# A feed-forward split in two parts by tokens: 384 tokens with plain products, 768 with Strassen's seven half-size products in the up projection

## The chip, the core and the metric

The kernel runs on one core of one Trainium2 chip, as one launch. The metric is the device time of that launch in microseconds, the median of three runs. The core's engines work in parallel, each through its own list of instructions in order: TensorE (PE, matrix products into PSUM), VectorE (DVE), ScalarE (ACT), GpSimd (POOL), and SyncE (SP), which issues the DMA transfers here.

## The reference, cut to what matters

One step of a hybrid backbone layer on 1024 latent tokens and 128 prompt tokens: a mixer (a bidirectional mLSTM branch beside a grouped-query attention branch), then a feed-forward of width 4096 on a model width of 1024. All is float32. The change is in the feed-forward, the second half of the layer:

```python
    x = layer_norm(ALPHA * x + g1 * mix, ln1_g, ln1_b)
    h = x * (1 + sc2) + sh2
    ff = jnp.square(jax.nn.relu(h @ w_up)) @ w_down
    x = layer_norm(ALPHA * x + g2 * ff, ln2_g, ln2_b)
```

`w_up` is 1024 x 4096 and `w_down` 4096 x 1024; `sh2`, `sc2` and `g2` come from a conditioning vector, one set for the latent tokens and one for the prompt.

## The kernel before, in words

The 1152 tokens are 9 tiles of 128 (eight latent, the last one the prompt), gathered in three groups of 384 for products that have tokens as columns. The program has four stages: input projection and mLSTM, attention, branch and output projections with the first layer norm, feed-forward.

Every float32 product is made of three: `split` (L69 to L71) copies an operand to a rounded high part on ScalarE (L70) and takes the difference as a low part on VectorE (L71); `mm3` (L73 to L78) multiplies high by high (L76), high by low (L77, L78). A weight goes through `wslot`: a load of 512 KB into one of the two `raw` buffers of the pool `rp`, then a split into one of four pairs of slots `wh`, `wl` of the pool `wp`. The next load into a `raw` buffer waits until both halves of the split, or whatever else reads it, are done.

The feed-forward runs over 16 blocks of 256 hidden columns. `up(fb)` (L1111) loads and splits 1024 x 256 of w_up (`w_pair`, two slots), and for each of three token groups and two halves of 128 hidden columns makes one PSUM tile u by 24 matmuls of 384 columns: 144 in a block. ScalarE takes relu out of PSUM (L1122), VectorE squares it (L1123), and a split gives the tiles ah and al. `down(fbs, parts, last)` (L1130) loads and splits 256 rows of w_down, and for each of 9 token tiles and two halves of the model width makes a tile d by 6 matmuls of 512 columns, 108 in a block, which VectorE adds to acc in SBUF (L1143; in the first block a copy, L1141). PSUM has three buffers for u and three for d. The loop is up(fb + 1), then down(fb), so that the vector work on one block's activations lies beside the next block's products.

The modulated, transposed activations h2T (high and low, one pair of tiles th, tl for each group of 384) stay in SBUF throughout. In the last block `residual` (L1158) turns acc into ALPHA * x1 + g2 * acc, with x1 loaded back from DRAM, one buffer of 512 KB. The last down takes blocks 14 and 15 together, 12 matmuls a tile; it scales by g2 (L1146), adds (L1147), takes statistics (L1148) and, one token tile behind, finishes the layer norm (`finish`, L1170: ScalarE L1179, VectorE L1180, GpSimd L1181, store).

The order of instructions on each engine is settled when the kernel is built, by a scheduler that goes by the program's dependencies, the pools' buffers and its own estimates of durations. So an operation may stand far from the place at which the program's text has it.

Of the kernel before, what the change touches and what calls it, by code (L numbers as in the profile page):

```python
# [12 lines left out]
ALU = mybir.AluOpType  # L13
# [21 lines left out]
def hybrid_step_kernel(  # L35
# [15 lines left out]
    def pool(stack, name, bufs=1, **kw):  # L51
        return stack.enter_context(tc.tile_pool(name=name, bufs=bufs, reuse_waits="tile", **kw))
# [10 lines left out]
    def load(out, in_):  # L63
        nc.sync.dma_start(out=out, in_=in_)
# [32 lines left out]
    def kview(w):  # L97
        return w.rearrange("(k p) n -> p k n", p=128)
# [860 lines left out]
    st3r = ctx.enter_context(ExitStack())  # L959
    st3 = ctx.enter_context(ExitStack())  # L960
    ps3t = pool(st3r, "ps3t", 2, space=PSUM, side="right")
# [95 lines left out]
        nc.gpsimd.tensor_tensor(out=y, in0=y, in1=gain, op=ALU.mult)  # L1057
# [18 lines left out]
    h2T = []  # L1076
    for s in range(NT):
        if s in (0, NS):
# [16 lines left out]
        x1s.append(xt)  # L1095
        if s:
            modulate2(s - 1)
    st3.close()

# [1 line left out]
    st4 = ctx.enter_context(ExitStack())  # L1101
    ps4 = pool(st4, "ps4", 3, space=PSUM)
    fp = pool(st4, "fp", 1)

    def ft(shape, tag, bufs=1, ty=F32):
        return fp.tile(list(shape), ty, tag=tag, bufs=bufs, name=tag)

    NFB = DFF // 256
    wdv = kview(w_down)

    def up(fb, mid=None, each=None):  # L1111
        w = w_pair(w_up, 256 * fb)
        ah = ft([128, 2, 1152], "ah", 2, F32R)
        al = ft([128, 2, 1152], "al", 2, F32R)
        for b in range(NTB):
            for m in range(2):
                if (b, m) == (1, 1) and mid:
                    mid()
                g = ps4.tile([128, 512], F32, tag="u", name="u4")
                mm3(g[:, 0:TB], [(w[m][k], (h2T[b][0][:, k, :], h2T[b][1][:, k, :])) for k in range(KT)])  # L1120
                r = ft([128, 512], "r", 2)[:, 0:TB]
                nc.scalar.activation(out=r, in_=g[:, 0:TB], func=AF.Relu)  # L1122
                nc.vector.tensor_tensor(out=r, in0=r, in1=r, op=ALU.mult)  # L1123
                sl = slice(b * TB, b * TB + TB)
                split(ah[:, m, sl], al[:, m, sl], r)
                if each:
                    each()
        return ah, al

    def down(fbs, parts, last):  # L1130
        ws = [(a, m, wslot([(0, wdv[:, 2 * fb + m:2 * fb + m + 1, :])], 1024)) for fb, a in zip(fbs, parts) for m in range(2)]
        for s in range(NT):
            ts_ = slice(128 * s, 128 * s + 128)
            if last:
                st = ft([128, 2, 6], "bst", 2)
            for half in range(2):
                cs = slice(512 * half, 512 * half + 512)
                g = ps4.tile([128, 512], F32, tag="d", name="d4")
                mm3(g[:], [((a[0][:, m, ts_], a[1][:, m, ts_]), (w[0][:, 0, cs], w[1][:, 0, cs])) for a, m, w in ws])
                if fbs[0] == 0:  # L1140
                    nc.vector.tensor_copy(out=acc[:, s, cs], in_=g[:])  # L1141
                elif not last:
                    nc.vector.tensor_tensor(out=acc[:, s, cs], in0=acc[:, s, cs], in1=g[:], op=ALU.add)  # L1143
                else:
                    tm = ft([128, 512], "r", 2)
                    nc.vector.tensor_tensor(out=tm[:], in0=g[:], in1=g2t[0 if s < NS else 1][:, cs], op=ALU.mult)  # L1146
                    nc.vector.tensor_tensor(out=acc[:, s, cs], in0=acc[:, s, cs], in1=tm[:], op=ALU.add)  # L1147
                    nc.vector.bn_stats(out=st[:, half, :], in_=acc[:, s, cs])  # L1148
            if last:
                if s:  # L1150
                    finish(s - 1, *fin)
                fin = ln_stats(st, ft)
        if last:
            finish(NT - 1, *fin)

    g2t = []

    def residual(s):  # L1158
        if not g2t:
            for g in range(2):  # L1160
                t = ft([128, D], f"g2{g}")
                load(t[:], gmod[1, g, :].partition_broadcast(128))
                g2t.append(t)
        x1 = ft([128, D], "x1")
        load(x1[:], x1d[s][:])
        y = acc[:, s, :]
        nc.vector.tensor_tensor(out=y, in0=y, in1=g2t[0 if s < NS else 1][:], op=ALU.mult)  # L1167
        nc.vector.scalar_tensor_tensor(out=y, in0=x1[:], scalar=ALPHA, in1=y, op0=ALU.mult, op1=ALU.add)  # L1168

    def finish(s, mv, rs):  # L1170
        out = y_sample[0, 128 * s:128 * s + 128, :] if s < NS else y_prompt[0]
        nmu = ft([128, 1], "nmu", 2)
        nc.vector.tensor_scalar(nmu[:], mv[:, 0:1], -1.0, None, ALU.mult)
        n = 1 if s < NS else 2
        for i in range(n):
            w = D // n
            cs = slice(w * i, w * i + w)
            y = acc[:, s, cs]
            nc.scalar.activation(out=y, in_=y, func=AF.Identity, bias=nmu[:])  # L1179
            nc.vector.scalar_tensor_tensor(out=y, in0=y, scalar=rs[:], in1=l2g[:, cs], op0=ALU.mult, op1=ALU.mult)  # L1180
            (nc.gpsimd if s < NS else nc.vector).tensor_tensor(out=y, in0=y, in1=l2b[:, cs], op=ALU.add)  # L1181
            store(out[:, cs], y)

    a = up(0, lambda: modulate2(NS))
    st3r.close()
    st4r = ctx.enter_context(ExitStack())
    accp = pool(st4r, "accp", 1, side="right")
    acc = accp.tile([128, NT, D], F32, name="acc")
    for fb in range(NFB - 2):
        nxt = up(fb + 1)  # L1190
        down([fb], [a], False)
        a = nxt
    todo = list(range(NT))

    def some():
        for _ in range(2):
            if todo:
                residual(todo.pop(0))

    b = up(NFB - 1, None, some)  # L1200
    while todo:
        some()
    l2 = tp.tile([128, 2, D], F32, tag="t", name="l2")
    l2g, l2b = l2[:, 0, :], l2[:, 1, :]
    load(l2g, ln2_g[0].partition_broadcast(128))
    load(l2b, ln2_b[0].partition_broadcast(128))
    down([NFB - 2, NFB - 1], [a, b], True)


# [48 lines left out]
```

## Time and profile before

| what | value |
|---|---|
| runs | 2469.79, 2470.90, 2470.94 us; median 2470.9 |
| the profiled execution's span | 2469.1 us |
| busy: TensorE, VectorE, ScalarE, GpSimd | 97%, 57%, 34%, 13% |
| first matmul of an up product | at 1651.6 us |
| one feed-forward block in mid-stage | 49.51 us |
| last matmul | at 2452.0 us |
| DMA | 264.77 MB, 107 GB/s over the span |

A row of the timeline has start, duration, engine, line, operation, output and inputs, and in brackets the idle time before it with what ended it. A row of the groups has line, engine, operation, shapes and count, then busy us and mean ns of one, then idle us before them with the releasers. A row of the windows has the stretch, its length, busy us of PE, PEld, DVE, ACT and POOL, the granted TensorE clock, the DMA share and GB/s. Matmuls are pipelined, so the durations listed for them overlap; their starts tell what one costs.

### The profile page before, as it was taken

To read this page: it belongs to the slowest core of one execution; us is meant where nothing else is said; L and a number is where in the kernel's file an instruction comes from. 1 tells how busy PE (TensorE), PEld (TensorE's weight loads), DVE (VectorE), ACT (ScalarE), POOL (GpSimd) and SP (SyncE) were. 2 spreads that over 40 slices of the span, in tenths; PEclk is the share of its full clock that TensorE was granted. 3 is DMA by queue.
4 is the path that set the end of the run, shared out by engine and by line. 5 is a ranking of instruction groups with operands and counts; after the bars stand their busy time and mean duration, and the time that the engine had idled before them with its cause. 6 is when DMAs were issued, how large, how long until landed. Compare 5 with 4: busy or idle time off the path is not lost. (4 is left out here: it accounts for less than half of the span.)

```text
span 2469.1 us, 35511 instructions
## 1 busy us (share of the span) xinstructions
PE 2387.7 (97%) x13485; PEld 2163.7 (88%) x13485; DVE 1399.7 (57%) x2625; ACT 843.8 (34%) x1844; POOL 312.3 (13%) x514
## 2 busy tenths in 40 slices
PE   6999998999999899899999999999999999999997
PEld 4888887788899899889999999888999899989985
DVE  5645635645654464378787345674445444544488
ACT  3323423534433243266666333132221122212221
POOL 1001100211110010134442000230000000000004
PEclk9999999999999999999999999999999999999998
DMA  7264447445654642520001655241111111111131
GB/s 266 87 206 152 148 120 198 138 125 146 196 165 145 183 148 95 104 72 17 16 16 58 216 188 189 93 141 35 52 35 52 35 52 35 51 35 52 35 120 77
DMA packets 211162, 264.77 MB, mean 107 GB/s; under 512 B 23760, under 2 KB 157984, under 8 KB 210992
## 3 DMA queue, kind: packets, MB, share of 16 engines
q1 hardware_dynamic: 210992, 262.51, 34.7%
q8 instruction: 106, 1.74, 0.3%
q14 instruction: 64, 0.52, 0.1%
HBM read 197.23 MB, written 65.21 MB: 106 GB/s over the span
## 5 line engine op out<-in xcount | busy, mean ns | idle before, releaser
L76 PE MATMUL g<-th,wh 128*128 128x384 f32 x1088 | 373.5, 343 | 8.7 <-DVE fm L246 8.7
L78 PE MATMUL g<-th,wl 128*128 128x384 f32 x1088 | 368.3, 338 | 0.0
L77 PE MATMUL g<-tl,wh 128*128 128x384 f32 x1088 | 366.7, 337 | 0.0
L70 ACT ACTIVATE wh<-raw 128x1024 fp32r<-128x1024 f32 x148 | 154.9, 1058 | 405.8 <-PE d L78 289.4
L76 PE MATMUL u<-th,wh 128*128 128x384 f32 x768 | 256.8, 335 | 0.8 <-ACT th L70 0.8
L77 PE MATMUL u<-tl,wh 128*128 128x384 f32 x768 | 256.7, 334 | 0.6 <-DVE tl L71 0.6
L78 PE MATMUL u<-th,wl 128*128 128x384 f32 x768 | 256.7, 334 | 0.0
L76 PE MATMUL g<-wh,th 128*128 128x512 f32 x600 | 241.1, 402 | 0.0
L77 PE MATMUL g<-wl,th 128*128 128x512 f32 x600 | 236.1, 394 | 0.7 <-DVE wl L71 0.7
L78 PE MATMUL g<-wh,tl 128*128 128x512 f32 x600 | 236.5, 394 | 0.0
L1143 DVE TENSOR_TENSOR acc<-acc,d 128x512 f32<-128x512 f32 x234 | 159.4, 687 | 119.6 <-PE d L78 119.6
L77 PE MATMUL d<-wl,ah 128*128 128x512 f32 x576 | 224.6, 390 | 2.3 <-DVE wl L71 2.3
L76 PE MATMUL d<-wh,ah 128*128 128x512 f32 x576 | 224.4, 390 | 1.8 <-DVE r L1146 1.6
L78 PE MATMUL d<-wh,al 128*128 128x512 f32 x576 | 224.4, 390 | 0.0
L76 PEld LDWEIGHTS g<-th,wh 128*128 128x128 f32 x1088 | 206.3, 190 | 17.5 <-DVE fm L246 9.0
L71 DVE TENSOR_TENSOR wl<-raw,wh 128x1024 fp32r<-128x1024 f32 x148 | 180.8, 1230 | 71.2 <-ACT wh L70 70.6
L78 PEld LDWEIGHTS g<-th,wl 128*128 128x128 f32 x1088 | 206.1, 189 | 0.4 <-issue 0.4
L77 PEld LDWEIGHTS g<-tl,wh 128*128 128x128 f32 x1088 | 206.4, 190 | 0.1
L1123 DVE TENSOR_TENSOR r<-r 128x384 f32<-128x384 f32 x96 | 53.5, 558 | 166.4 <-ACT r L1122 166.3
L76 PEld LDWEIGHTS u<-th,wh 128*128 128x128 f32 x768 | 144.1, 188 | 1.7 <-ACT th L70 1.1
L77 PEld LDWEIGHTS u<-tl,wh 128*128 128x128 f32 x768 | 144.2, 188 | 1.5 <-DVE tl L71 1.0
L78 PEld LDWEIGHTS u<-th,wl 128*128 128x128 f32 x768 | 144.1, 188 | 0.0
(307 smaller groups left out, 4675.4 us busy)
## 6 DMA issues: line engine op xcount, KB each, us to landing
raw<-in_w_in_dram SPq DMA_DIRECT2D x44, 512.0 KB
kvt<-kvd SPq DMA_DIRECT2D x64, 257.0 KB
raw<-in_w_mod_dram SPq DMA_DIRECT2D x32, 512.0 KB
raw<-in_w_up_dram SPq DMA_DIRECT2D x32, 512.0 KB
raw<-in_w_down_dram SPq DMA_DIRECT2D x32, 512.0 KB
kvd<-kvs SPq DMA_DIRECT2D x36, 257.0 KB
uw<-ud SPq DMA_DIRECT2D x72, 128.0 KB
bs<-st SPq DMA_DIRECT2D x32, 258.0 KB
```

The costliest lines, as they stand in the source:

```text
L70: nc.scalar.activation(out=hi, in_=src, func=AF.Copy)
L71: nc.vector.tensor_tensor(out=lo, in0=src, in1=f(hi), op=ALU.subtract)
L76: nc.tensor.matmul(out, lhsT=ah, rhs=bh, start=start and i == 0, stop=False)
L77: nc.tensor.matmul(out, lhsT=ah, rhs=bl, start=False, stop=False)
L78: nc.tensor.matmul(out, lhsT=al, rhs=bh, start=False, stop=stop and i == n - 1)
L1123: nc.vector.tensor_tensor(out=r, in0=r, in1=r, op=ALU.mult)
L1143: nc.vector.tensor_tensor(out=acc[:, s, cs], in0=acc[:, s, cs], in1=g[:], op=ALU.add)
```

## The change

The helper lines of split become L71 to L73 and those of mm3 L78 to L80, since two constants come in above them; apart from stage 3's order of tokens, only stage 4 differs.

**Token order.** Stage 3 takes the tiles in the order 0, 1, 2, 6, 7, 8, 3, 4, 5.

**First part, tokens 0 to 2.** `up_plain` (L1194) has 48 matmuls a block, and down 36. Two up blocks precede the first down. All 16 blocks run so, the last two downs together, and the three tokens are finished then, in mid-kernel, with `residual` and `finish` as parameters of which accumulator and pool they use.

**Activation forms.** Between, `act_forms` prepares the seven activation matrices of Strassen's scheme for the other 768 tokens: a11 and a12 are the two halves in depth of the middle token group, s1 and s4 overwrite the halves of the last group, s2, s3 and a22 get tiles of their own. GpSimd adds high to low for each quarter (L1121) and subtracts (L1127), 32 operations of 128 x 384 in all, and ScalarE and VectorE split the 16 results.

**Second part, tokens 3 to 8.** All 16 blocks of w_up and w_down are loaded and split again. `up_forms` makes the seven weight forms of a block from two raw halves: GpSimd combines (L1281, four operations of 128 x 512), and each form is split into one of three rotating places of the tile uf. `up_halves` (L1330) makes seven products of 12 matmuls of 384 columns, 84 a block, in PSUM banks x, y and z; x and y have one buffer each, z is one of u's three. VectorE makes sums out of PSUM (L1339), GpSimd one (L1361), ScalarE relu and square (L1325, L1326). `down` has 72 matmuls a block, and the last of them finishes six tokens.

**Residual.** acc times g2 goes from VectorE to GpSimd (L1132), x1 is loaded in halves of 256 KB.

The core of the diff:

```diff
+NFB = 16
+SORD = (0, 1, 2, 6, 7, 8, 3, 4, 5)
...
+        for k in range(4):
+            full = []
+            for nm in ("a11", "s1", "a12", "s4"):
+                t = mk([128, TB], "v" + nm)
+                nc.gpsimd.tensor_tensor(out=t[:], in0=f(acts[nm][0][:, k, :]), in1=f(acts[nm][1][:, k, :]), op=ALU.add)
+                full.append(t)
+                yield
+            b11, b12, b21, b22 = full
+            t3 = mk([128, TB], "vs3")
+            for dst, x, y, nm in ((t3, b22, b12, "s3"), (b11, b12, b11, "s1"), (b22, b22, b11, "s2"), (b21, b21, b22, "a22")):
+                nc.gpsimd.tensor_tensor(out=dst[:], in0=x[:], in1=y[:], op=ALU.subtract)
+                split(acts[nm][0][:, k, :], acts[nm][1][:, k, :], dst[:])
+                yield
...
+    def some_forms():
+        next(forms, None)
+        next(forms, None)
+
+    T0 = (0, 1, 2)
+    for fb in range(NFB - 3):
+        down(fat, acc0, T0, [fb], [a], down_w([fb]), None, None, False)
+        a, nxt = nxt, up_plain(fb + 2, some_forms)
...
+    ORDER = ("a11", "s2", "s1", "s3", "s4", "a12", "a22")
+    BANK = "xyzyzxy"
...
+        s1 = comb(0, a21, a22, ALU.add)
+        s2 = comb(1, s1, a11, ALU.subtract)
+        yield form(a11)
+        yield form(s2)
+        yield form(s1)
+        s3 = comb(2, a11, a21, ALU.subtract)
+        yield form(s3)
+        s4 = comb(3, a12, s2, ALU.subtract)
+        yield form(s4)
+        yield form(a12)
+        yield form(a22)
...
+            for k in range(4):
+                for i, (x, y) in enumerate(((wh, bh), (wh, bl), (wl, bh))):
+                    nc.tensor.matmul(o, lhsT=x[:, k, :], rhs=y[:, k, :], start=fresh and k == 0 and i == 0,
+                                     stop=k == 3 and i == 2, skip_group_check=True)
+            if j == 0:
+                nc.scalar.activation(out=tmp("u1"), in_=o, func=AF.Copy)
+            elif j == 1:
+                tsum(tmp("u2"), u["u1"], o)
+            elif j == 2:
+                nc.scalar.activation(out=tmp("v"), in_=o, func=AF.Copy)
+            elif j == 3:
+                u3 = ft([128, TB], "r", 2)[:]
+                tsum(u3, u["u1"], o)
+                nc.gpsimd.tensor_tensor(out=u["v"], in0=u3, in1=u["v"], op=ALU.add)
+                half_out(a, 1, 1, u["v"])
...
+    for fb in range(NFB - 2):
+        nxt = up_halves(pre, aa[(fb + 1) % 2], lambda: None)
+        ws = down_w([fb])
+        pre = up_begin(fb + 2)
+        down(ft, acc, T1, [fb], [a], ws, None, None, False)
+        a = nxt
```

Three places of the order matter below. The first is VectorE at the second down product of the feed-forward; before, the add of its first group (d4_18517) stands behind the square of the last hidden half (r_18500) and two weight splits:

```order
L71 TENSOR_TENSOR al_18324<-r_18470,ah_18323 128x384
L71 TENSOR_TENSOR wl_18664<-raw_18661,wh_18663 128x1024
L71 TENSOR_TENSOR wl_18670<-raw_18667,wh_18669 128x1024
L1123 TENSOR_TENSOR r_18500<-r_18500 128x384
L1143 TENSOR_TENSOR acc_17960<-acc_17960,d4_18517 128x512
L71 TENSOR_TENSOR al_18324<-r_18500,ah_18323 128x384
```

In the changed kernel, the same place (the add of the first group of down(1) is d4_18088; va, vs are GpSimd's combined activations, tf and tl the low parts of the forms):

```order
L73 TENSOR_TENSOR tl_17342<-va11_18616,th_17341 128x384
L73 TENSOR_TENSOR al_18007<-r_18033,ah_18006 128x384
L73 TENSOR_TENSOR tfs3l_17747<-vs3_18758,tfs3h_17746 128x384
L73 TENSOR_TENSOR wl_18139<-raw_18136,wh_18138 128x1024
L73 TENSOR_TENSOR tfs2l_17745<-vs4_18652,tfs2h_17744 128x384
L73 TENSOR_TENSOR tfa22l_17749<-va12_18650,tfa22h_17748 128x384
L1203 TENSOR_TENSOR r_18067<-r_18067 128x384
L1170 TENSOR_TENSOR acc0_17930<-acc0_17930,d4_18088 128x512
L73 TENSOR_TENSOR wl_18145<-raw_18142,wh_18144 128x1024
L73 TENSOR_TENSOR al_18007<-r_18067,ah_18006 128x384
L1170 TENSOR_TENSOR acc0_17930<-acc0_17930,d4_18096 128x512
```

The splits of activation forms have moved in ahead of the square and the add. On ScalarE, at the same place of the changed kernel, the relu that feeds that square stands behind the split of the fourth s1 quarter:

```order
L72 ACTIVATE wh_18138<-raw_18136 128x1024
L72 ACTIVATE tfs2h_17744<-vs4_18652 128x384
L72 ACTIVATE tfa22h_17748<-va12_18650 128x384
L72 ACTIVATE th_17341<-va11_18905 128x384
L1202 ACTIVATE r_18067<-u4_18042 128x384
```

Ahead of it stand splits that need all but the last four of GpSimd's 32 operations. The third place is VectorE in a block of the second part, from the last activations of an up product into the adds of a down product (raw_21884 is half of a W_down block, wth the weight forms s1 and s2):

```order
L1339 TENSOR_TENSOR u1_21519<-u1_21519,psy_21524 128x384
L73 TENSOR_TENSOR uf_19924<-wth_21650,uf_19924 128x512 x2
L1170 TENSOR_TENSOR acc_20113<-acc_20113,d4_21660 128x512
L73 TENSOR_TENSOR aal_20109<-r_21629,aah_20108 128x384
L1170 TENSOR_TENSOR acc_20113<-acc_20113,d4_21668 128x512
L73 TENSOR_TENSOR wl_21887<-raw_21884,wh_21886 128x1024
L1170 TENSOR_TENSOR acc_20113<-acc_20113,d4_21676 128x512
L1170 TENSOR_TENSOR acc_20113<-acc_20113,d4_21684 128x512
```

GpSimd in the same block (raw_21646 and raw_21648 are the two halves of the next w_up block):

```order
L1281 TENSOR_TENSOR wtl_21651<-raw_21646 128x512
L1361 TENSOR_TENSOR x_21555<-r_21571,x_21555 128x384
L1281 TENSOR_TENSOR wth_21650<-raw_21646,raw_21648 128x512
L1281 TENSOR_TENSOR wth_21650<-wth_21650,raw_21646 128x512
L1281 TENSOR_TENSOR wtl_21651<-raw_21648,wth_21650 128x512
```

Before, in a block of the feed-forward, GpSimd had nothing, and the split of a W_down block stood ahead of all the adds of its product.

More of the change, by code (lines that the diff above doesn't have):

```diff
@@ L1075, in hybrid_step_kernel @@
     load(l1b[:], ln1_b[0].partition_broadcast(128))
[L1076 to L1078 removed]
+    h2T = {}
+    for i, s in enumerate(SORD):
+        if s in (0, NS) or SORD[i - 1] == NS:
             load(g1t[:], gmod[0, 0 if s < NS else 1, :].partition_broadcast(128))
@@ L1102, in hybrid_step_kernel @@
     ps4 = pool(st4, "ps4", 3, space=PSUM)
[L1103 to L1108, printed above, removed]
+    tf = pool(st4, "tf", 1)
+    fs = pool(st4, "fs", 1)
     wdv = kview(w_down)
[L1111 to L1133, printed above, removed]
+    acts = {}
+    for nm in ("s2", "s3", "a22"):
+        acts[nm] = tuple(tf.tile([128, 4, TB], F32R, tag=nm + e, name="tf" + nm + e) for e in "hl")
+    def act_forms(mk):
+        acts["a11"] = tuple(t[:, 0:4, :] for t in h2T[1])
+        acts["a12"] = tuple(t[:, 4:8, :] for t in h2T[1])
+        acts["s1"] = tuple(t[:, 0:4, :] for t in h2T[2])
+        acts["s4"] = tuple(t[:, 4:8, :] for t in h2T[2])
+        for k in range(4):
[11 more added lines that the diff above has]
+                yield
@@ L1134, in down, with down_w @@
+    def down_w(fbs):
+        return [wslot([(0, wdv[:, 2 * fb + m:2 * fb + m + 1, :])], 1024) for fb in fbs for m in range(2)]
+    def down(mk, acc, toks, fbs, parts, ws, g2, l2, split_last):
+        last = g2 is not None
+        ws = [(parts[i // 2], i % 2, w) for i, w in enumerate(ws)]
+        fin = None
+        for i, s in enumerate(toks):
+            ts_ = slice(128 * i, 128 * i + 128)
             if last:
-                st = ft([128, 2, 6], "bst", 2)
+                st = mk([128, 2, 6], "bst", 2)
@@ L1149, in down @@
             if last:
-                if s:
-                    finish(s - 1, *fin)
-                fin = ln_stats(st, ft)
+                if fin:
+                    finish(mk, *fin, 1)
+                fin = (acc[:, i, :], s, l2, *ln_stats(st, mk))
         if last:
[L1154 to L1182, printed above, removed]
@@ L1184, in hybrid_step_kernel, with load_l2 @@
-    a = up(0, lambda: modulate2(NS))
-    st3r.close()
[L1186 to L1193, printed above, removed]
+            finish(mk, *fin, 2 if split_last else 1)
+    def load_l2(l2):
+        load(l2[0], ln2_g[0].partition_broadcast(128))
+        load(l2[1], ln2_b[0].partition_broadcast(128))
@@ new lines, in hybrid_step_kernel, with fat, up_plain @@
+    s4a = ctx.enter_context(ExitStack())
+    fa = pool(s4a, "fa", 1)
+    def fat(shape, tag, bufs=1, ty=F32):
+        return (fs if tag in "rx" else fa).tile(list(shape), ty, tag=tag, bufs=bufs, name=tag)
+    def up_plain(fb, each):
+        w = w_pair(w_up, 256 * fb)
+        ah = fat([128, 2, TB], "ah", 2, F32R)
+        al = fat([128, 2, TB], "al", 2, F32R)
+        for m in range(2):
+            g = ps4.tile([128, 512], F32, tag="u", name="u4")
+            mm3(g[:, 0:TB], [(w[m][k], (h2T[0][0][:, k, :], h2T[0][1][:, k, :])) for k in range(KT)])
+            r = fat([128, TB], "r", 2)[:]
+            nc.scalar.activation(out=r, in_=g[:, 0:TB], func=AF.Relu)
+            nc.vector.tensor_tensor(out=r, in0=r, in1=r, op=ALU.mult)
+            split(ah[:, m, :], al[:, m, :], r)
+            each()
+        return ah, al
@@ new lines, in hybrid_step_kernel, with fft @@
+    forms = act_forms(lambda shape, tag: tt4.tile(list(shape), F32, tag=tag, name=tag))
+    def some_forms():
[5 more added lines that the diff above has]
+        a, nxt = nxt, up_plain(fb + 2, some_forms)
+    for _ in forms:
+        pass
+    s4t.close()
+    s4f = ctx.enter_context(ExitStack())
+    ff = pool(s4f, "ff", 1, side="right")
+    def fft(shape, tag, bufs=1, ty=F32):
+        return (fs if tag in "rx" else ff).tile(list(shape), ty, tag=tag, bufs=bufs, name=tag)
@@ L1195, in some @@
+    g2a = fft([128, D], "g20")
+    load(g2a[:], gmod[1, 0, :].partition_broadcast(128))
+    l2a = fft([128, 2, D], "l2a")
+    load_l2((l2a[:, 0, :], l2a[:, 1, :]))
+    todo = list(T0)
     def some():
@@ new lines, in up_begin @@
+    def up_begin(fb):
+        gen = up_forms(fb)
+        return gen, [next(gen) for _ in range(3)]
+    ws = down_w([NFB - 2, NFB - 1])
+    pre = up_begin(0)
+    down(fft, acc0, T0, [NFB - 2, NFB - 1], [a, nxt], ws, [g2a], (l2a[:, 0, :], l2a[:, 1, :]), False)
+    s4f.close()
+    s4b.close()
+    s4a.close()
+    fp = pool(st4, "fp", 1)
+    aa = [fp.tile([128, 2, 768], F32R, tag="aa" + e, name="aa" + e) for e in "hl"]
+    aa = ((aa[0][:], aa[1][:]), (ab[:, 0:2, :], ab[:, 2:4, :]))
+    ar = pool(s4r, "ar", 1, side="right")
@@ L1201, in hybrid_step_kernel @@
+    todo = list(enumerate(T1))
+    nxt = up_halves(pre, aa[1], some1)
     while todo:
-        some()
+        some1()
     l2 = tp.tile([128, 2, D], F32, tag="t", name="l2")
[L1204 to L1207, printed above, removed]
+    l2 = (l2[:, 0, :], l2[:, 1, :])
+    load_l2(l2)
+    down(ft, acc, T1, [NFB - 2, NFB - 1], [a, nxt], down_w([NFB - 2, NFB - 1]), [g[:] for g in g2b], l2, True)
```

136 lines of the change are left out of this document (122 added, 14 removed).

## The prediction

> **What bounds the kernel now.** First the page's busy shares, then one stretch of the feed-forward by windows (span us, then busy us of each engine, granted clock, DMA share, GB/s):
>
> ```profile
> span 2469.1 us, 35511 instructions
> PE 2387.7 (97%) x13485; PEld 2163.7 (88%) x13485; DVE 1399.7 (57%) x2625; ACT 843.8 (34%) x1844; POOL 312.3 (13%) x514
> 1800.00:1900.00 100.00, 100.00 (x511) 91.50 (x511) 47.45 (x69) 20.61 (x34) 0.00 (x0) 1.00 0.13 43
> ```
>
> TensorE never rests there, VectorE is half free, GpSimd does nothing. The list of groups gives durations, the timeline the distance from one matmul to the next:
>
> ```profile
> L76 PE MATMUL u<-th,wh 128*128 128x384 f32 x768 | 256.8, 335 | 0.8 <-ACT th L70 0.8
> L70 ACT ACTIVATE wh<-raw 128x1024 fp32r<-128x1024 f32 x64 | 66.2, 1057 | 315.3 <-PE d L78 289.4 <-PE u L77 18.1 <-DMA raw<-in_w_up_dram 7.5
> L71 DVE TENSOR_TENSOR wl<-raw,wh 128x1024 fp32r<-128x1024 f32 x64 | 77.0, 1222 | 23.7 <-ACT wh L70 23.7
> L71 DVE TENSOR_TENSOR al<-r,ah 128x384 fp32r<-128x384 f32 x96 | 53.5, 558 | 45.1 <-ACT ah L70 45.0
> L1143 DVE TENSOR_TENSOR acc<-acc,d 128x512 f32<-128x512 f32 x234 | 159.4, 687 | 119.6 <-PE d L78 119.6
> ...
> 1850.04 0.33 PE L77 MATMUL u<-tl,wh 128*128 128x384 f32 x1
> 1850.21 0.33 PE L78 MATMUL u<-th,wl 128*128 128x384 f32 x1
> ...
> 1852.98 0.39 PE L76 MATMUL d<-wh,ah 128*128 128x512 f32 x1
> 1853.21 0.40 PE L77 MATMUL d<-wl,ah 128*128 128x512 f32 x1
> ```
>
> The listed means (335 ns) overlap; what a 384-column matmul costs is 0.1735 us from start to start, a 512-column one 0.2275 (0.23 here). The chain of waits shows one block of 256 hidden columns, from one down product to the next:
>
> ```profile
> 1952.16 0.23 PE d L76
> ...
> 2001.66 0.23 PE d L76
> ...
> 2051.17 0.23 PE d L76
> ```
>
> 49.51 us, which is 144 x 0.1735 + 108 x 0.2275 = 25.0 + 24.6: matmul time with nothing between. What is taken from TensorE's list is gained, and whatever the change makes TensorE wait for is lost in full.
>
> **Removed: an eighth of two thirds of the up matmuls.** For tokens 3 to 8, a block has 7 products of 12 matmuls instead of 8, 84 for 96. Over 16 blocks that is 192 x 0.1735 = **33.3 us off**. The down products stay at 1728 matmuls. A steady block of 768 tokens should take 14.6 (up) + 72 x 0.2275 = 16.4 (down) = 31.0 us, one of 384 tokens 8.3 + 8.2 = 16.5.
>
> **The price of GpSimd work.** No row of before has a 128x384 add on GpSimd; these bracket it, and show what happens when VectorE runs an operation with two SBUF inputs beside it:
>
> ```profile
> L815 POOL TENSOR_TENSOR pql<-pq,pqh x2: 1285/1288/1290, 1029.1 to 1055.1; 128x512 fp32r<-128x512 f32 x2
> L547 POOL TENSOR_TENSOR pm<-uw,mask x36: 733/741/1656, 152.7 to 957.5; 128x256 f32<-128x256 f32 x36
> ...
> 2418.84 2.40 POOL L1181 TENSOR_TENSOR acc<-acc,l 128x1024 f32<-128x1024 f32 x1 [2.31 <-DVE acc L1180]
> ...
> 2419.40 2.39 DVE L1147 TENSOR_TENSOR acc<-acc,r 128x512 f32<-128x512 f32 x1
> ...
> 1643.87 1.22 DVE L71 TENSOR_TENSOR wl<-raw,wh 128x1024 fp32r<-128x1024 f32 x1
> ...
> 1644.09 3.25 POOL L1057 TENSOR_TENSOR m<-m 128x1024 f32<-128x1024 f32 x1 [0.98 <-issue]
> ```
>
> Between 0.74 (256 columns) and 1.29 (512) I take 1.01, and 0.09 between operations: 1.10 each. VectorE's L1147 took 2.39 us and ended 0.55 after GpSimd's operation did; it has 512 elements a row, as the 0.69 of L1143. In the last pair GpSimd came second and took 3.25, for the 2.40 of the same shape. They exclude one another.
>
> **Added at the front: the activation forms.** The order puts all 32 GpSimd operations of act_forms at the start of the first phase, between the first and the third down product, with their splits on ScalarE and VectorE in between. The add of the first group of down(1) (d4_18088, second order fence of the change) stands on VectorE behind the square of r_18067; that waits for ScalarE's relu of u4_18042, which stands behind the split th_17341<-va11_18905, the product of the 28th of those operations. Counted from the start of down(0): GpSimd starts near 6.2 (estimated from what stands on VectorE up to the last token's split: two weight splits of 1.22, that split of the same size, four transposed pieces, a square), 28 x 1.10 = 30.8 puts its 28th end at 37.0, relu, square and add are over by 39. VectorE's two-input operations in that stretch (14 splits of 0.56, 3 of 1.22: 11.5 us) would, if they all excluded GpSimd, make it 51. TensorE would end down(0) and up(2) at 16.5 and has three PSUM buffers for d, so the fourth group, at 16.5 + 3 x 1.37 = 20.6, is the first to need that add: 18 to 30 us late. The splits of the last forms stand between the adds that follow, about 3 more. The bounds are 18 (nothing of that exclusion, no later hold) and 33; the pairs of rows above speak for exclusion, and I take **29 lost**. Page "SBUF — State Buffer" of the Trainium skill (section "SBUF: two separate sides") says that GpSimd and a VectorE operation with two SBUF inputs take a shared port pair as an exclusive lock, the later one waiting for the whole operation; the rows agree (2.39 for 0.69), and by that rule alone the sum would lie 4 us higher, with 33 here.
>
> **Added between the phases.** What follows a last down product is seen in the tail of before:
>
> ```profile
> 2403.68 0.69 DVE L1146 TENSOR_TENSOR r<-d,g 128x512 f32<-128x512 f32 x1 [0.35 <-PE d L78]
> ...
> 2452.02 0.39 PE L78 MATMUL d<-wh,al 128*128 128x512 f32 x1
> ...
> 2464.57 1.29 DVE L1181 TENSOR_TENSOR acc<-acc,l 128x512 f32<-128x512 f32 x2
> ```
>
> VectorE needs 62 us for 9 tokens, 6.8 each, where TensorE needs 24 x 0.2275 = 5.5. Now three tokens end in mid-kernel: VectorE falls 3 x 1.3 = 4 behind, then does most of the last token (6.8) and loses about 2.4 to one GpSimd operation before the sum u2 (L1339), for which the fourth product's bank waits: 13 after the last matmul, of which three products cover 6.2, so 7 lost. Four W_down slots are wanted at once and two raw buffers are there: the later pair costs about 4 (a load and a split, below, less cover); the first two blocks start late with their forms, 3 more. **14 lost**, 6 to 20 as these overlap or add.
>
> **Added in each steady block of the second phase.** Raw weights pass through two buffers. The order shows that one keeps the second half of w_up from block to block, the other takes W_down twice and w_up's first half in turn. What a load takes from issue to use:
>
> ```profile
> 1650.36 0.38 SPq L64 DMA_DIRECT2D raw<-in_w_up_dram  x1
> ...
> 1654.03 1.06 ACT L70 ACTIVATE wh<-raw 128x1024 fp32r<-128x1024 f32 x1 [2.19 <-DMA raw<-in_w_up_dram]
> ...
> 2226.10 1.51 SPq L64 DMA_DIRECT2D raw<-in_w_up_dram  x2
> 2227.00:2228.00 1.00, 1.00 (x8) 1.00 (x7) 0.21 (x1) 0.00 (x0) 0.00 (x0) 1.00 0.66 153
> 2228.00:2229.00 1.00, 1.00 (x8) 1.00 (x7) 0.00 (x0) 0.49 (x1) 0.00 (x0) 1.00 0.99 351
> ```
>
> 3.67 us in the first pair; in the second the bytes of one 512 KB load (153 + 351 KB) are in after 2.9. Counted from the start of an up product, the chain runs: fourth product over, 8.6; form a22 split on ScalarE (0.6) and VectorE (0.7, held by GpSimd's add of v, 0.9), 10.85; load of w_up's second half, 14.5; GpSimd's two sums s1 and s2 (1.29 each), 17.1; only then is the other buffer free, and W_down's load comes at 20.8; split 1.06 + 1.22, 23.1; and behind that split on VectorE (L73 wl_21887) stands the add of the third down group, over at 23.9. The sixth group needs its PSUM buffer at 14.6 + 5 x 1.37 = 21.4. **2.5 us a block, 13 blocks: 32 lost.** With 2.9 a load it is 1.0; with VectorE's adds and forms ahead held once more, 3.7: 13 to 48. This cover is gone at any load over 2.4 us.
>
> **The rest.** The second W_up and W_down passes add 32 MB; the DMA share of 0.13 leaves room, nothing. Residual products on GpSimd, relu's square on ScalarE (20.61 of 100 busy): nothing on the path. Two up blocks of 384 tokens ahead of the first down hide the last token's transposes, where TensorE waited 0.8 + 0.6 us: −1.4. The tail has the same length, six tokens instead of nine to fall behind: −1, give or take 4.
>
> **Sum.** −33.3 + 29 + 14 + 32 − 1.4 − 1 = +39. The profiled execution, at 2469.1 us of span, is 1.8 under the median of 2470.9, to which I add: **2510 us**. All low ends together (18, 6, 13, −5) give −3, 2468; all high ones (33, 20, 48, +3) +69, 2540.
>
> **Rivals.** (1) Faster: the loads come in under 2.4 us. Then the buffer chain ends before 21.4 and the steady blocks cost nothing; with the front at 22 and the change of phase at 6, −33.3 + 28 − 2.4 = −8: 2463. For it: only one load at a time is out, and DMA is at 0.13. Against: 2.9 in the barest case above, and 3.67. The point is 2.4 us a load. 0.12, of which a third lands within 5 us of before.
> (2) The front is half covered: a GpSimd operation of 384 columns takes 0.74 and excludes nothing; 29 shrinks to 8: 2489. For it, the 0.74 of 256 columns; 6.2 + 28 x 0.74 + 2 = 29 is then still 8 over the 20.6. Against, the 1.29 of 512. 0.12.
> (3) The clock falls after each wait. Near the program's start it did (windows: clock before DMA share):
>
> ```profile
> 27.34 1.06 PE L355 MATMUL pc<-ident,xt 128*128 128x128 f32 x8 [2.03 <-DMA xt<-in_x_sample_dram]
> ...
> 30.19 0.52 PE L76 MATMUL go<-th,wgh 128*128 128x384 f32 x1
> 30.51 0.52 PE L77 MATMUL go<-tl,wgh 128*128 128x384 f32 x1
> ...
> 30.00:35.00 5.00, 3.93 (x19) 3.54 (x17) 0.95 (x2) 0.63 (x1) 0.00 (x0) 0.74 1.03 408
> PE u L76 <- ACT th L70: 0.8, 1, 0.8
> PE u L77 <- DVE tl L71: 0.6, 1, 0.6
> ...
> 1670.00:1675.00 5.00, 4.21 (x23) 3.89 (x23) 2.25 (x3) 1.00 (x3) 0.00 (x0) 1.00 0.00 0
> ```
>
> About ten matmuls went 0.32 apart, 1.5 us lost after a wait of 2.03; after waits of 0.80 and 0.64 the clock stayed 1.00. If all 13 steady waits and a few of the long ones bring it, 14 x 1.5 = 21 more: 2531. 0.14. The Trainium skill's page "TensorE: Matmul & The Clock Gate" (Part 1) halves the clock only after an idle window of some 3.4 us, for about as long; by that rule only the two long waits, at the front and between the phases, are followed by it, and the sum would be 3 higher, 2513, by an estimate of 1.7 each.
> (4) The change does not save: products accumulated on shared banks take as long as eight. +33 on the sum, 2543. The order counts 84 matmuls of 384 columns, as those of before: 0.03.
>
> **How the numbers follow.** Forecast 0.59, the rivals 0.12, 0.12, 0.14, 0.03. A run tells 0.2% (4.9 us) from no change. Faster: two thirds of (1) and the lowest end of the forecast, 0.12. Same: the rest of (1) and a little of that end, 0.05. Slower: 0.83. The range leaves out a tenth below 2467, most of (1), and some 0.07 above 2546, where (3) meets the high bounds.
>
> **What would show it.** TensorE's idle list with 25 to 33 us near the start of the feed-forward for d, ended by VectorE's L1170; 2 to 3 us in each later block on L1170 of the third group, its VectorE chain leading through L73 wl to a W_down load; the steady block at 33.5, not 31.0; 192 fewer 384-column matmuls at 0.1735. It is wrong if steady blocks are 31 us long, if GpSimd's 128x384 takes under 0.6, or if no wait of over 10 us stands at the front.

## The result, and the profile after

The changed kernel takes 2510.87 us (median of 4 runs, 2508.51 to 2513.13) against 2470.35 for before beside it: ratio 1.0162, 95% interval 1.0148 to 1.0177. It is slower by 1.6%. The profiled execution spans 2506.7 us:

```profile
span 2506.7 us, 36075 instructions
PE 2377.3 (95%) x13293; PEld 2136.6 (85%) x13293; DVE 1553.9 (62%) x2785; ACT 991.4 (40%) x2100; POOL 489.4 (20%) x635
```

TensorE has 192 instructions fewer and is busy for 10 us less, and yet the kernel is longer: TensorE waits. All that it waited for in the feed-forward, from the list of waits (us in total, times, longest):

```profile
PE d L78 <- DVE acc L1170: 33.0, 20, 16.1
PE psy L1350 <- DVE u L1339: 7.9, 2, 7.0
PE d L78 <- DVE acc L1168: 6.0, 3, 4.1
PE d L78 <- ACT wh L72: 2.4, 1, 2.4
PE d L80 <- DVE ab L73: 1.3, 1, 1.3
PE psx L1350 <- ACT r L1325: 1.2, 1, 1.2
PE psy L1350 <- DVE uf L73: 1.1, 1, 1.1
PE d L79 <- DVE wl L73: 0.9, 1, 0.9
PE d L78 <- ACT ab L72: 0.7, 1, 0.7
```

Before, four such rows came to 5.3 us; here the nine come to 54.5, of which 50.2 are for VectorE. Idle time as listed leaves out what a slow clock takes. So I also sum, from the first up matmul to the last down matmul, what lies between two matmul starts beyond 0.1735 or 0.2275 us, and call these the gaps: 7.5 us before, 77.8 after. That stretch grew from 800.5 to 840.2 us; what follows the last matmul stayed (17.1 and 17.4). The 77.8 lie in four places: 24.4 at the front of the feed-forward, none in the other blocks of the first part, 24.8 at the change of phase, 18.5 in eleven steady blocks, 10.0 at the end.

**The front.** GpSimd's first operation of the activation forms and that of the fourth s1 quarter, then what follows the latter on ScalarE and VectorE, then TensorE:

```profile
1672.17 1.87 POOL L1121 TENSOR_TENSOR va<-th,tl 128x384 f32<-128x384 f32 x1 [12.80 <-issue]
...
1706.36 1.19 POOL L1127 TENSOR_TENSOR va<-vs,va 128x384 f32<-128x384 f32 x1
```

```profile
1707.58 0.52 ACT L72 ACTIVATE th<-va 128x384 fp32r<-128x384 f32 x1 [2.03 <-POOL va L1127]
1708.01 0.47 ACT L1202 ACTIVATE r<-u 128x384 f32<-128x384 f32 x1
...
1708.51 0.56 DVE L1203 TENSOR_TENSOR r<-r 128x384 f32<-128x384 f32 x1 [1.82 <-ACT r L1202]
1708.98 0.68 DVE L1170 TENSOR_TENSOR acc<-acc,d 128x512 f32<-128x512 f32 x1
...
1709.72 0.80 PE L78 MATMUL d<-wh,ah 128*128 128x512 f32 x1 [16.15 <-DVE acc L1170]
```

Sum, split, relu, square, add, matmul, link by link as the order had it. In the trace that quarter is the 27th operation, not the 28th, and five follow it. The 27 took 35.4 us, 1.31 each.

**A steady block.** The products of this block begin at 2172.64 and those of the next at 2205.21, 32.57 us where the matmuls need 31.0:

```profile
2172.64 0.33 PE L1350 MATMUL psx<-th,uf 128*128 128x384 f32 x1
...
2181.67 0.69 DVE L73 TENSOR_TENSOR uf<-raw,uf 128x512 fp32r<-128x512 f32 x1
...
2186.14 1.30 POOL L1281 TENSOR_TENSOR wth<-raw 128x512 f32<-128x512 f32 x1 [2.90 <-DMA raw<-in_w_up_dram]
2187.52 1.50 POOL L1281 TENSOR_TENSOR wth<-wth,raw 128x512 f32<-128x512 f32 x1
...
2189.82 1.92 DVE L73 TENSOR_TENSOR uf<-wth,uf 128x512 fp32r<-128x512 f32 x2
2191.67 0.67 DVE L1170 TENSOR_TENSOR acc<-acc,d 128x512 f32<-128x512 f32 x1
...
2192.40 0.50 PE L78 MATMUL d<-wh,aah 128*128 128x512 f32 x1 [0.89 <-DVE acc L1170]
...
2192.57 1.06 ACT L72 ACTIVATE wh<-raw 128x1024 fp32r<-128x1024 f32 x1 [0.84 <-DMA raw<-in_w_down_dram]
2193.66 1.23 DVE L73 TENSOR_TENSOR wl<-raw,wh 128x1024 fp32r<-128x1024 f32 x1 [0.26 <-ACT wh L72]
2194.81 1.88 DVE L1170 TENSOR_TENSOR acc<-acc,d 128x512 f32<-128x512 f32 x3
2205.21 0.33 PE L1350 MATMUL psx<-th,uf 128*128 128x384 f32 x1
```

The split of form a22 ends at 2182.36 and frees the raw buffer, GpSimd has the next half at 2186.14, its two sums end at 2189.02, and the two forms stand ahead of the first add: the fourth group waits 0.9 us for it. The second link (the split of W_down, ahead of the third add) costs some 0.3 us more.

**The change of phase.** VectorE, GpSimd beside it, and TensorE's fourth product:

```profile
1952.91 1.28 DVE L1148 SCALAR_TENSOR_TENSOR acc<-acc,brs,l2a 128x1024 f32<-128x1024 f32 x1 [1.94 <-POOL brs L1050]
1954.12 0.68 DVE L1174 TENSOR_TENSOR acc<-acc,x 128x512 f32<-128x512 f32 x1
1954.72 2.83 DVE L73 TENSOR_TENSOR uf<-wt,uf 128x512 fp32r<-128x512 f32 x1
...
1958.07 0.53 DVE L1339 TENSOR_TENSOR u<-u,psy 128x384 f32<-128x384 f32 x1
...
1954.28 2.72 POOL L1149 TENSOR_TENSOR acc<-acc,l2a 128x1024 f32<-128x1024 f32 x1 [1.40 <-DVE acc L1148]
...
1958.66 0.69 PE L1350 MATMUL psy<-tfs3h,uf 128*128 128x384 f32 x1 [7.05 <-DVE u L1339]
```

A split of 0.69 us takes 2.83 beside GpSimd's add, and the sum u2 behind it lets the fourth product go 7 us late.

### The profile page after: what moved, and what is told of

It is laid out like the page before. It is cut to its first block, busy times and chain, and to the rows that moved or that the text cites. A ratio compares the mean times of both kernels' runs of the same rounds, so it can differ in the third digit from the quotient of the medians.

```text
span 2506.7 us, 36075 instructions
## 1 busy us (share of the span) xinstructions
PE 2377.3 (95%) x13293; PEld 2136.6 (85%) x13293; DVE 1553.9 (62%) x2785; ACT 991.4 (40%) x2100; POOL 489.4 (20%) x635
## 4 chain that ended last, share of the span: by engine, by line
PE 71%; DMA 9%; DVE 9%; POOL 4%; ACT 3%; issue 2%; SPq 0%; DVEq 0%; ACTq 0%; POOLq 0%
PE g L78 12%; PE g L80 12%; PE g L79 12%; PE d L78 3%; PE d L79 3%; PE d L80 3%; PE psy L1350 3%; PE t L872 2%; DMA raw<-in_w_down_dram 2%; DMA raw<-in_w_up_dram 2%; PE u L78 2%; PE u L79 2%; PE u L80 2%; POOL wth L1281 1%; DVE wl L73 1%
## 5 line engine op out<-in xcount | busy, mean ns | idle before, releaser
L78 PE MATMUL g<-th,wh 128*128 128x384 f32 x1088 | 373.2, 343 | 7.4 <-DVE fm L248 7.4
L80 PE MATMUL g<-th,wl 128*128 128x384 f32 x1088 | 367.7, 338 | 0.0
L73 DVE TENSOR_TENSOR wl<-raw,wh 128x1024 fp32r<-128x1024 f32 x180 | 224.5, 1254 | 76.0 <-ACT wh L72 75.0
L78 PE MATMUL g<-wh,th 128*128 128x512 f32 x600 | 241.1, 402 | 0.9 <-ACT xq L643 0.8
L80 PE MATMUL g<-wh,tl 128*128 128x512 f32 x600 | 236.4, 394 | 0.0
L78 PEld LDWEIGHTS g<-th,wh 128*128 128x128 f32 x1088 | 205.9, 189 | 16.2 <-DVE fm L248 7.7
L80 PEld LDWEIGHTS g<-th,wl 128*128 128x128 f32 x1088 | 205.7, 189 | 0.4 <-issue 0.4
L1170 DVE TENSOR_TENSOR acc<-acc,d 128x512 f32<-128x512 f32 x234 | 156.4, 683 | 67.2 <-PE d L80 67.2
L78 PEld LDWEIGHTS g<-wh,th 128*128 128x128 f32 x600 | 113.1, 188 | 26.3 <-issue 3.8
L80 PEld LDWEIGHTS g<-wh,tl 128*128 128x128 f32 x600 | 113.1, 189 | 23.5
L79 PEld LDWEIGHTS g<-wl,th 128*128 128x128 f32 x600 | 113.4, 189 | 20.3 <-DVE wl L73 0.4
L72 ACT ACTIVATE ph<-t 128x384 fp32r<-128x384 f32 x192 | 91.0, 493 | 70.6 <-PE t L872 70.2
L248 DVE COPY fm<-g 128x384 f32<-128x384 f32 x96 | 53.2, 555 | 99.6 <-PE g L80 99.3
L73 DVE TENSOR_TENSOR pl<-t,ph 128x384 fp32r<-128x384 f32 x192 | 104.8, 549 | 9.1 <-ACT ph L72 7.1
L872 PE MATMUL t<-ident,pe 128*128 128x128 f32 x576 | 96.2, 276 | 6.5 <-DVE pl L73 5.5
L78 PE MATMUL d<-wh,ah 128*128 128x512 f32 x192 | 77.2, 402 | 23.1 <-DVE acc L1170 16.5
L861 POOL TENSOR_SCALAR pe<-pe,rs 128x1152 f32<-128x1152 f32 x64 | 78.8, 1230 | 54.9 <-DVE rs L860 27.0
L78 PE MATMUL d<-wh,ab 128*128 128x512 f32 x192 | 77.6, 404 | 10.5 <-DVE acc L1170 9.5
```

Of the source, the lines that this page charges most:

```text
L72: nc.scalar.activation(out=hi, in_=src, func=AF.Copy)
L73: nc.vector.tensor_tensor(out=lo, in0=src, in1=f(hi), op=ALU.subtract)
L78: nc.tensor.matmul(out, lhsT=ah, rhs=bh, start=start and i == 0, stop=False)
L79: nc.tensor.matmul(out, lhsT=ah, rhs=bl, start=False, stop=False)
L80: nc.tensor.matmul(out, lhsT=al, rhs=bh, start=False, stop=stop and i == n - 1)
L248: nc.vector.tensor_copy(out=st[:], in_=g[:, 0:TB])
```

## The experiments

The first up matmul stands between 1648.4 and 1654.5 us in these profiles, though nothing ahead of it was changed. Where a few us matter I therefore give, beside the time, the stretch from that matmul to the last one (after: 840.2). All ratios are to before.

### The activation forms spread over eight blocks

```diff
-                split(acts[nm][0][:, k, :], acts[nm][1][:, k, :], dst[:])
+                with tc.issue_after(gate[0].ins), tc.issue_after(gate[1].ins):
+                    split(acts[nm][0][:, k, :], acts[nm][1][:, k, :], dst[:])
```

`gate` holds the two instructions of the last activation split of the block in whose text the call stands. GpSimd follows, since its five buffers come free only with the splits.

> Same work as the changed kernel; the splits of the activation forms are queued on ScalarE and VectorE behind the block of the first part in whose text they stand, so GpSimd's 32 operations spread over eight blocks. If the 16.3 us wait at 1693 us of the changed kernel comes from the burst standing ahead of down(1)'s first add, that wait and the slow clock behind it go (about 18 us, 2493 us). If it comes from the amount of GpSimd and VectorE work, which exclude one another wherever they stand, the loss is spread over the blocks and the time stays within 5 us of 2511.

Measured: 2497.84 us, ratio 1.0114 (1.0097 to 1.0131), 13.0 less than after. TensorE's waits from 1660 to 1731 us, here and, in the second fence, in the changed kernel:

```profile
PE d L78 <- DVE acc L1170: 4.1, 1, 4.1
PE d L78 <- DVE acc L1172: 0.7, 2, 0.4
```

```profile
PE d L78 <- DVE acc L1170: 16.5, 2, 16.1
PE d L78 <- DVE acc L1168: 4.1, 1, 4.1
```

The wait of 16 us is gone; the one of 4.1, for the first copy out of PSUM (L1170 here, L1168 there), is another thing and stays. It was the place of the burst. A little came back: 2.7 us in the blocks to which the work moved, which had none.

### The forms without GpSimd

```diff
+            for src_, nm in (("s4", "s3"), ("s1", "s1"), ("s4", "s2"), ("a12", "a22")):
+                split(acts[nm][0][:, k, :], acts[nm][1][:, k, :], f(acts[src_][0][:, k, :]))
```

This takes the place of all 32 GpSimd operations of act_forms.

> Leaves out GpSimd's 32 sums and differences of the activation forms: the 16 splits remain and take one high part each as input, so the outputs of tokens 3 to 8 are not the reference's. If the 28 GpSimd operations ahead of the add are the cause at the front, the wait of 16.3 us goes, 2493 us. If the splits themselves (16 of 0.53 us on ScalarE, 16 of 0.56 on VectorE, all standing early) crowd out the add, most of it stays, over 2503 us.

Measured: 2494.36 us, 1.0095 (1.0080 to 1.0110); the front keeps one wait, 4.7 us, for the copy. The 16 splits, as early as before, crowd out nothing: GpSimd's operations were the length of that chain.

### The weight forms later on VectorE

```diff
-        pre = up_begin(fb + 2)
         down(ft, acc, T1, [fb], [a], ws, None, None, False)
+        with tc.issue_after(adds[-10].ins):
+            pre = up_begin(fb + 2)
```

`adds` lists the adds of the down products, twelve in a block; `adds[-10]` is the third.

> Same work; on VectorE the first three weight forms of the block after next are queued behind the third add of a down product, not ahead of its first; the order then puts the splits of W_down later too (behind the seventh add). If the steady waits (1.0 + 0.3 us a block) come from what stands ahead of those adds in VectorE's list, they go: 13 x 1.6 = 20 us, 2490 us. If the chain of loads through two raw buffers itself has no room in a block of 31 us, the waits come back at a later add or at the next product's forms, and no more than 5 us are won.

Measured: 2498.47 us, 1.0116 (1.0101 to 1.0131). Blocks are 31.4 us long; from 2044 to 2390 us, eleven blocks, TensorE's waits are those of the first fence, the changed kernel's in such blocks those of the second:

```profile
PE d L78 <- DVE acc L1171: 1.9, 6, 0.6
```

```profile
PE d L78 <- DVE acc L1170: 11.9, 14, 1.8
```

So 1.2 us a block came from what stood ahead of the adds, and the chain of loads has room in a block of 31 us. The gain is 12 us, not 20: 0.4 a block remains, and the gaps at the end of the stage grew by 2.7.

### Only the split of W_down later

```diff
+        with tc.issue_after(adds[-7].ins):
+            ws = down_w([fb])
```

> Same work; only the split of W_down is queued behind the sixth add, the weight forms stay ahead of the first. My chain (load, sums s1 and s2, load, split of W_down, third add) makes the split the last link: 1.3 us a block should go, 17 us, if it were so. By the changed kernel's rows the wait of 1.0 us comes at the fourth group, behind the weight forms, and only 0.3 at the sixth, behind the split: 13 x 0.3 = 4 us, 2507 us.

Measured: 2510.48 us, 1.0164 (1.0149 to 1.0180), which by itself is no difference. In the trace the blocks are 32.1 us instead of 32.6, and the stretch is 834.6, 5.6 less; the first up matmul stood 4.5 us later. The wait of 1.0 us a block stays. The first link, the weight forms, decides; the chain of the prediction ended in the wrong one.

### Without GpSimd's sums s1 and s2

```diff
-        s1 = comb(0, a21, a22, ALU.add)
-        s2 = comb(1, s1, a11, ALU.subtract)
+        s1, s2 = (a22, a22) if fb else (comb(0, a21, a22, ALU.add), comb(1, a22, a11, ALU.subtract))
```

> Leaves out GpSimd's sums s1 and s2 of the weight forms from the second block on (both forms are split from the raw quarter a22 itself, s4 is a12 less that quarter; the outputs of tokens 3 to 8 are not the reference's). In the changed kernel these two, 2.8 us, stand between the load of w_up's second half and the two forms ahead of the first add, and beside them VectorE's splits take 1.0 to 1.1 us for 0.55. If they are a link of the chain that ends in the 1.0 us wait, the wait goes and the blocks fall from 32.6 to about 31.2: 18 us less, 2493 us. If the load alone or VectorE's own work is what comes last there, the blocks stay over 32.2, 2506 us.

Measured: 2492.45 us, 1.0088 (1.0073 to 1.0103); blocks of 31.4. VectorE in one of them:

```profile
2179.53 0.54 DVE L73 TENSOR_TENSOR ab<-r,ab 128x384 fp32r<-128x384 f32 x1
2180.00 0.68 DVE L73 TENSOR_TENSOR uf<-raw,uf 128x512 fp32r<-128x512 f32 x1
2180.60 0.67 DVE L1170 TENSOR_TENSOR acc<-acc,d 128x512 f32<-128x512 f32 x1
```

In the changed kernel the same kinds of split, beside the sums, took 1.01, 1.09 and 1.92 us for two. The two GpSimd operations are the link, by their length and by what they do to the splits beside them; this run doesn't divide the two. That the same 1.2 us go when the forms merely stand later says that neither had to cost TensorE anything.

### The finish of two token tiles later, and without GpSimd

```diff
+    with tc.issue_after(sums[1].ins):
+        for h in held:
+            finish(fft, *h, 1)
```

The first of two kernels: `held` has the second and third tile, `sums` the sums of the first Strassen product.

> Same work; the layer-norm finish of the second and third token tile is queued on VectorE behind the second of the sums of the first Strassen product, not ahead of the first. The sum u2 then stands behind one scale, one add and one split only: the wait of 7.2 us before the fourth product should fall to about 2, 2506 us. If u2 waits for its weight form or its PSUM bank instead, the wait stays at 7.

```diff
-            (nc.gpsimd if n == 1 else nc.vector).tensor_tensor(out=y, in0=y, in1=l2[1][:, cs], op=ALU.add)
+            (nc.gpsimd if n == 1 and s > 2 else nc.vector).tensor_tensor(out=y, in0=y, in1=l2[1][:, cs], op=ALU.add)
```

The second.

> Same work; in the finish of tokens 0 to 2 the last add (1024 columns) is on VectorE instead of GpSimd. In the changed kernel a 0.69 us form split takes 2.83 beside GpSimd's add, and VectorE waits 1.94 for a small GpSimd operation behind another. If this exclusion is the larger part of the 7.2 us wait, it falls by 3 or more although VectorE gets 1.2 us of work a token; 2508 us. If it is VectorE's amount of work, the wait stays or grows.

Measured: 2510.64 us, 1.0162 (1.0145 to 1.0179), and 2507.36 us, 1.0151 (1.0136 to 1.0166). TensorE's waits from 1940 to 2000 us in the first, in the second:

```profile
PE psy L1347 <- ACT uf L72: 3.9, 1, 3.9
PE d L78 <- DVE acc L1170: 3.1, 1, 3.1
PE psy L1347 <- DVE u L1336: 2.1, 1, 2.1
PE psx L1347 <- ACT uf L72: 1.5, 1, 1.5
```

```profile
PE psy L1350 <- DVE u L1339: 4.1, 1, 4.1
PE d L78 <- DVE acc L1168: 2.9, 1, 2.9
```

The second has four smaller rows besides: 1.6 and 0.8 for weight forms, 0.5 and 0.2. Both hit the wait for u2, from 7.0 to 2.1 and to 4.1. In the first kernel the second block's weight forms, which were hidden behind it, are the next wait, 3.9, and the total hardly moves: a repair is worth what is late next. In the second the wait fell by 2.9 although VectorE got the add as well: beside it, GpSimd's add, off the path by itself, had cost that much.

### Two parts with plain products

In this kernel `up_halves` makes 96 plain matmuls a block, in the way of the first part, with no forms and no sums.

```diff
-    forms = act_forms(lambda shape, tag: tt4.tile(list(shape), F32, tag=tag, name=tag))
+    forms = iter(())
...
-        pre = up_begin(fb + 2)
```

> The two parts by tokens stay, but the second part has plain products: 96 matmuls a block, no activation forms, no weight forms, no sums. If the losses are those of the forms (front 18 us, steady blocks about 20, sum u2 and what follows it at the change of phase about 11), they go while 33.3 us of matmuls come back: 2511 - 49 + 33 = 2495, at best 2483, where only the wait for the first copy (4.3) and for W_down at the change of phase (4) remain over before. If the division into two parts costs by itself (two passes over the weights, a finish in mid-kernel), it stays over 2505 us.

Measured: 2486.27 us, 1.0063 (1.0046 to 1.0079), between the two figures. The gaps sum to 23.8 us against 7.5 before and 77.8 after. So the division into two parts costs some 16 us by itself, Strassen's forms and sums 54, with the slow clock behind their waits, and its matmuls save 33. The profiled execution was the slowest of the four (2492.12), with its first up matmul 5.4 us later than in the changed kernel; the gaps leave that out.

### All repairs

Forms spread, weight forms later, finish later and on VectorE, and:

```diff
-                    nc.vector.tensor_copy(out=acc[:, i, cs], in_=g[:])
+                    nc.scalar.activation(out=acc[:, i, cs], in_=g[:], func=AF.Copy)
```

> Same work, all repairs together: activation forms spread over eight blocks, weight forms queued behind the third add (but not in the first and last blocks), the finish of two token tiles behind the second sum and its last add on VectorE, and ScalarE instead of VectorE copies the first down product of each part out of PSUM. If the waits are independent and each repair takes its own: -14 (front), -4 (copy), -13 (steady), -6 (change of phase) from 2511, 2474 us, within 5 us of before; if they hide one another, under half of that, over 2492.

Measured: 2476.15 us, 1.0020 (1.0009 to 1.0030). The first four had given 13.0, 12.4, 0.2 and 3.5 us alone; together, with the copy, which had no run of its own, they give 34.7. The next kernel has all these, with the finish behind the last sum, one W_down slot more and the residual behind the adds; beside it stands the same with the weight forms later in two more blocks:

```diff
-    ws = down_w([NFB - 2, NFB - 1])
+    ws = down_w([NFB - 2])
...
+    w2 = [ab[:].rearrange("p a b -> p (a b)")[:, 1024 * e:1024 * e + 1024] for e in range(2)]
+    split(w2[0], w2[1], raw[:])
...
+    with tc.issue_after(sums[3].ins):
...
-            residual(ft, acc[:, i, :], s, g2b[-1][:])
+            with tc.issue_after(adds[-1].ins):
+                residual(ft, acc[:, i, :], s, g2b[-1][:])
```

> All repairs of the run before, with three more, same work: the finish of two token tiles waits behind the last sum of the first Strassen block (VectorE rows of that run show it ahead of the second block's weight forms, 7 us, before a wait of 4.0); the third W_down half of the first part's last product is split into the tile ab, which nothing uses until then, so that only the fourth is late (waits of 2.7 and 1.4); the residual of the second part stands on VectorE behind all adds of down(13) (wait of 2.3). If these three are the causes of those waits, 3 + 3 + 2 us go: 2468 us, just under before. If what is behind them comes next, as it did when only the finish was moved, 2474 or more.

> As the kernel beside it, with the weight forms queued behind the third add in the first and the last block of the second part too. If those two blocks lose as the steady ones did, 1 to 2 us less than beside; if the forms are then late for the product that follows at once, 1 to 3 more.

Measured: 2468.17 us, 0.9992 (0.9983 to 1.0001), and 2468.99 us, the same ratio and interval. No difference from before, nor between the two; the wait of 2.3 us at block 13 had stayed, behind a W_down split, and so had that for W_down (2.8). The last kernel therefore has the edits below, puts the weight forms of block 13 behind the adds as well, and loads the first W_down block of the first part's last product ahead of the last up product (`ws = down_w([NFB - 2])`, not shown):

```diff
-        nc.gpsimd.tensor_tensor(out=acc_s, in0=acc_s, in1=g2, op=ALU.mult)
+        (nc.vector if s < 3 else nc.gpsimd).tensor_tensor(out=acc_s, in0=acc_s, in1=g2, op=ALU.mult)
...
+    with tc.issue_after(adds[-6].ins):
+        ws = down_w([NFB - 2, NFB - 1])
```

> All repairs, and three more, same work: acc times g2 of the first three tokens is on VectorE instead of GpSimd (there a 0.68 us operation took 2.87 beside GpSimd's), the first W_down block of that part's last product is loaded ahead of the last up product, and the last W_down splits and the weight forms of block 13 stand behind the adds of down(13) (waits of 1.5 and 2.3). If these place the waits rightly, 3 to 5 us less than the 2468 of the kernel before it, 2464 us and faster than before by 0.25%; if others take their place, 2467 or more.

Measured: 2468.56 us against 2471.51 for before beside it, ratio 0.9986 (0.9977 to 0.9995). It beats the changed kernel by 42 us; the 0.14% against before are half of what was expected and less than the 0.2% that the prediction counted as no change. The kernel before it had 2468.17 against 2469.95, so these last edits are not shown to have won anything. From the first up matmul to the last one it takes 796.1 us, the kernel before it 796.6 and before 800.5. Its gaps sum to 33.9 us, as those of the kernel before it (34.8). The wait for W_down went, but one of 2.2 for VectorE's scaling (L1178) came in the same product, and at the end of the stage others took the place of that at block 13; these are not settled.

## Why the prediction was right

- **Matmuls.** 192 fewer, at the same distance from start to start, so 33.3 us as said. The listed busy time fell by 10 only, since matmuls at the slow clock (0.63 for 0.39) and those behind a wait (0.50) are listed longer.
- **The front: 29 forecast, 24.4 measured.** The mechanism is the one forecast. The exclusion of GpSimd and VectorE shows: 1.31 us an operation, where undisturbed ones took 0.99 to 1.02 and the forecast without exclusion had 1.10; and they were 27, not 28. The add was over 43.0 us after the start of down(0), between the bounds of 39 and 51. TensorE came to it at 26.7 instead of 20.6, since it had already lost 4.3 in a wait for the first copy, which I had not listed, and 1.6 to a slow clock. Of the 24.4, some 16.6 are that add, 4.3 that copy, 3.4 slow clock.
- **Between the phases: 14 forecast, 24.8 measured.** The sum u2 came out as worked (7 forecast, 7.2) and so did W_down (4, and 3.8). Mis-sized was "the first two blocks start late with their forms, 3 more": 6.0 in the first two up and down products, and only 1.1 of them for a form itself, the others for a relu, a sum and two copies that came late. The slow clock, which I had kept for a rival, is 5.0 of the rest.
- **Steady blocks: 32 forecast, 21 measured** (13 x 1.6; two of the 13 blocks also lie in the stretches counted above as the change of phase and the end). The failed step is "2.5 us a block": each link came about 1 us sooner than reckoned (the split of a22 over at 9.7 for 10.85, the sums at 16.4 for 17.1, W_down split at 22.3 for 23.1), since VectorE got there before GpSimd's add and made that wait instead. And the sixth group was the wrong place: the weight forms ahead of the first add delay the fourth group by 1.0, and little is left for the sixth.
- **Rivals.** Loads of 3.8 and 3.5 us, nowhere near 2.4, closed the first. The second's 0.74 us operations were 1.31. The third, a slow clock after every wait, is refuted for the steady waits of 1 us. But the sum had the slow clock at nothing, and there were seven slow stretches in the feed-forward, of 1.5 to 1.8 us each and 11.6 in all: 3.4 at the front, 5.0 between the phases, 3.3 at the end.

The total, +39 forecast and +40 measured, owes its closeness to errors that cancel: −5, +11, −11, and the end of the stage, put at −1, where the gaps grew by some 5 (5.5 before, 10.0 after) and whose waits I didn't take apart. The sign rests on none of them: with any one of the three terms at its low end and the others as measured, the sum stays above +20.

## What to carry to other kernels

Fewer matmuls are worth their time only where the work that feeds them finds its place: here 33 us of products were bought with 54 us of gaps, most of them from operations that stood ahead of an add or a sum in VectorE's list without being urgent. After a change, read in the order what stands ahead of whatever frees PSUM, and queue behind it what isn't needed soon. Here that took back 42 us with the same arithmetic, together with a few operations moved to another engine and one more place for a W_down half. Take each repair's worth from what is late next, not from the wait that it removes.

## What the runs showed of the hardware

The granted clock halved after a wait of 2.16 us and did not after one of 1.81. Windows of the changed kernel behind the latter and the former (busy us of PE, PEld, DVE, ACT and POOL, then clock), with the matmuls:

```profile
2127.20:2129.70 2.50, 2.50 (x11) 2.07 (x12) 2.07 (x4) 1.06 (x1) 0.00 (x0) 1.00 0.00 0
2426.60:2430.00 3.40, 3.40 (x8) 2.68 (x9) 3.40 (x4) 0.35 (x1) 2.76 (x1) 0.50 0.71 220
```

```profile
2127.09 0.50 PE L78 MATMUL d<-wh,aah 128*128 128x512 f32 x1 [1.81 <-DVE acc L1170]
2127.43 0.39 PE L79 MATMUL d<-wl,aah 128*128 128x512 f32 x1
...
2426.53 0.73 PE L78 MATMUL d<-wh,ab 128*128 128x512 f32 x1 [2.16 <-DVE acc L1170]
2427.05 0.63 PE L79 MATMUL d<-wl,ab 128*128 128x512 f32 x1
2427.48 0.63 PE L80 MATMUL d<-wh,ab 128*128 128x512 f32 x1
```

After 1.81 only the first matmul took longer (0.34 to the next start, for 0.23); after 2.16 seven or eight went 0.43 apart, 1.6 us lost.

The length of the wait alone does not decide. In the run with the finish later, a wait of 3.06 us (1995.97 to 1999.03) left the clock at 1.00, and in the changed kernel two waits of 0.89 and 1.14 us (up to 1973.43 and 1975.16) were followed by a halved one. In the feed-forward, the clock of each trace changes only at instants that are whole multiples of 3.41 us apart. Three such stretches follow: the first two are of the run with the finish later and hold the wait of 3.06, the third is of the changed kernel and holds the two short ones:

```profile
1993.97:1997.39 3.42, 2.00 (x9) 1.31 (x7) 2.38 (x2) 1.68 (x3) 3.23 (x3) 1.00 0.15 54
1997.39:2000.80 3.41, 1.77 (x8) 1.47 (x9) 3.27 (x6) 1.06 (x1) 0.00 (x0) 1.00 0.25 100
1972.65:1976.07 3.42, 1.49 (x7) 1.21 (x8) 3.42 (x6) 2.78 (x6) 1.31 (x1) 1.00 0.43 153
```

The wait of 3.06 was cut in two, with TensorE busy for over half of each stretch; in the third it was busy for 1.49, and the next stretch was slow. The feed-forward of all fourteen traces agrees, counted from the starts of the matmuls: a stretch at full clock with 1.8 us or more of idle time was followed by a slow one, one with less than 1.7 was not, and between these both occur. No run was made to test this.

The Trainium skill's page "TensorE: Matmul & The Clock Gate" (Part 1) puts the halving behind an idle window of some 3.4 us; here shorter waits sufficed. The slow stretches lasted 3 to 4 us, which agrees with the page.
